# One decoder layer with two token mixers, on one core: C21's block product ahead of C12's, single-bank PSUM tiles, and the first MLP pair's operands made ahead

## The chip, the cores and the metric

The kernel runs on one core of a Trainium2 chip. The metric is the device time of one execution in microseconds (us). TensorE (PE) does the matmuls, VectorE (DVE) and ScalarE (ACT) the elementwise work, GpSimd (POOL) elementwise work on SBUF, and SyncE (SP) issues all the transfers of the parts treated here, in one queue and in order.

## The reference

One layer on x, 1024 positions by 1024 features, all in float32:

```python
h = rmsnorm(x, mix_norm)
q, k, v, su, sv, g_a, g_b = split(h @ w_in)
y_att = sliding_window_attention(q, k, v, q_norm, k_norm, sinks)
y_sgu = chunked_spatial_gating(su, sv, sgu_norm, w_s, b_s)
merged = sigmoid(g_a) * (y_att @ w_oa) + sigmoid(g_b) * (y_sgu @ w_ob)
x = x + merged @ w_out
z = rmsnorm(x, ffn_norm) @ w_up              # 1024 x 5632
zc = conv_b + three causal taps of z          # depthwise over positions
gate, val = split(zc)
x = x + (silu(gate) * val) @ w_down
```

## The kernel before

A float32 number is split into a high and a low part (h, l), so that one product of operands is three matmul passes: high by high, high by low, low by high. ACT makes the high part (`copy_hi`, L87), and DVE or POOL subtracts it from the value to get the low part (L984 and L1315 among others). The large products (the gates, `merged @ w_out`, the MLP's up and down projections) are moreover cut into 2x2 blocks, and are computed with seven products of blocks instead of eight, on sums of blocks: on the left A11, A12, A22 and the sums S1 to S4, on the right B11, B21, B22 and the sums T1 to T4.

TensorE's order is written out by hand; the other engines take their instructions in the order of the program. What a matmul waits for follows from its operands and its PSUM tile. PSUM has eight banks of 512 float32 columns. In the part that matters here four of them are two tiles of 128x1024 in the pool psA, and four are two such tiles in psC. `PS` hands out tiles from the rotating list `psum["P"]`, so that two tiles come from one pool and the next two from the other.

The stages, in order:

- **Gates.** `gate_pair(c, prev)` for c = 1 to 7 computes one block column of both gates in seven products (`Blocks.prod`, L1024, 12 matmuls each) and adds the partial sums with DVE. `gate_out` applies tanh and stores the result (`dth`); `last_sum` of the pair before and `scale` come first on DVE.
- **Sum units.** `sums_step` makes sums of weights that later stages read: a unit of kind "o" (four DVE adds of 128x256, of `wout`) or "u" (two of 128x512, of `wup`). A unit is a load into one of two buffers `ls`, the adds (L620), and a store of the result (L1089 or L1096). `UNITS` gives the order. The step also issues a later unit's load. These steps are called three times per gate pair and beside some of the branches.
- **Branches.** 16 jobs (`branch(n)`), each 24 matmuls (L91, L93) of an attention or gating output by a column block of `w_oa` or `w_ob` (`wj`), followed by a DVE product with the stored tanh (`th`, loaded by `th_load` two branches ahead).
- **Out stage.** 14 groups, two for each of the products M1 to M7 in `OUT`, each 24 matmuls (L1456) into four half tiles of `X` (psC) or `Yb` (psA). Behind a group, `main` adds, stores and splits: `half_add` (L1312) adds the residual block from `acs`, `end_c11`, `end_c22`, `end_c12` and `end_c21` finish one block of the new x each, and make the right operands of the MLP from it (`hi`, `lo`, `lo_gain`). `ahead` issues what later groups and the first MLP pair need.
- **MLP.** 22 pairs: pair n computes a gate and a value column of 128 with the seven products, then the convolution (L1525), tanh and product (L1548, L1549). `first_pair` is written out on its own, as it starts on operands that the out stage is just finishing; its products stood in the order A11B11, S1T1, S3T3, A12B21, S2T2, S4B22, A22T4. The second pair's product A11B11 and the sums of squares for the RMS norm (L1504) follow, then `fast_pair` for the rest.
- **Down projection.** `mms` (L1812), again seven products in groups, into four tiles `pd` (`X`, the pool psD, which takes the banks of psC) and four half tiles `pdy` (`Yb`, psA).

Of the kernel before, what the change touches and what calls it, by code (L numbers as in the profile page):

```python
# [41 lines left out]
def body(ctx, tc, nc, a):  # L42
# [103 lines left out]
    psA = ctx.enter_context(tc.tile_pool(name="psA", bufs=2, space=bass.MemoryType.PSUM, reuse_waits="tile"))  # L146
# [977 lines left out]
    def gate_pair(c, prev):  # L1124
# [16 lines left out]
        sums_step()  # L1141
# [15 lines left out]
        sums_step()  # L1157
# [15 lines left out]
        if c > 1:  # L1173
            sums_step()
# [43 lines left out]
    def branch(n):  # L1218
        br, c = B_ORDER[n]

        def main(w):
# [16 lines left out]
            if n % 2 == 0 or n in (5, 9):  # L1238
                sums_step()
# [3 lines left out]
    def m_split(n, ks, src):  # L1243
        if n not in rt:
            rt[n] = (U if n in ("B21", "B22") else Y)("r" + n, R, [128, 2, 4, 512])
        copy_hi(rt[n][:, 0, ks, :], src)
        nc.vector.tensor_tensor(rt[n][:, 1, ks, :], src, rt[n][:, 0, ks, :].bitcast(F), op=ALU.subtract)
# [21 lines left out]
    for n in range(16):  # L1269
# [4 lines left out]
    OUT = (("M1", "B11", 0), ("M2", "B21", 1), ("M6", "T2", 0), ("M7", "T3", 2), ("M5", "T1", 3), ("M3", "B22", 1),  # L1274
           ("M4", "T4", 3))
# [5 lines left out]
    def open_out():  # L1281
# [8 lines left out]
        pools["ng2"] = fp.tile([128, 8], F, name="ng2")  # L1290
        nc.vector.tensor_scalar(pools["ng2"], g2, -1.0, None, op0=ALU.mult)
# [47 lines left out]
    def copies():  # L1339
        for d in range(4):  # L1340
            nc.scalar.copy(Yb[d], X[d])

    def end_c11():
        t = acs["C11"]
        for d in range(4):
            half_add(Yb[d], Yb[d], t[:, d, :])
            nc.scalar.copy(t[:, d, :], Yb[d])
            x2_store("C11", d)
            hi("B11", d, Yb[d], gain(d))
            if d:  # L1350
                lo_gain("B11", d - 1, Yb[d - 1], gain(d - 1))
        lo_gain("B11", 3, Yb[3], gain(3))
# [4 lines left out]
    def end_c22():  # L1357
        t = acs["C22"]
        sqt = Y("sqt", F, [128, 2, 4, 512])[:, 0]
        sq2 = pools["sq2"][:, H]  # L1360
        for d in range(4):
# [3 lines left out]
            nc.scalar.activation(sqt[:, d, :] if d else sq2, t[:, d, :], AF.Square)  # L1365
            if d:
                nc.gpsimd.tensor_tensor(sq2, sq2, sqt[:, d, :], op=ALU.add)
        for d in range(4):
            lo_gain("B22", d, t[:, d, :], gain(4 + d))

# [5 lines left out]
    def end_c12():  # L1376
        t, h11, h22 = acs["C12"], acs["C11"], acs["C22"]
        tr = Y("traw", F, [128, 2, 4, 512])
        traw.append(tr)

        def late(d):
            lo("T1", d, X[d])
            nc.vector.tensor_tensor(tr[:, 1, d, :], h22[:, d, :], X[d], op=ALU.subtract)  # L1383
# [603 lines left out]
```

## Time and profile before

| | |
|---|---|
| median of 3 runs | 1236.7 us (1235.47 to 1239.26) |
| profiled execution | 1236.46 us, span 1234.8 us |
| granted TensorE clock, mean | 0.987 |
| busy: PE, DVE, ACT, POOL | 96%, 75%, 46%, 48% of the span |
| stages | gate pairs 246.6 to 394.7, branches to 487.6, out stage to 572.3, first pair to 612.2, down projection from 1019.1 |

Times in the trace are counted from the start of the span. An engine's row has its start, its duration, the line of the code, the operation with output and inputs, the tile shapes and the number of instructions merged into the row; in brackets stands the idle time before it, and what ended that.

### The profile page before, as it was taken

How to read it: one execution, taken by the hardware profiler on the slowest of the kernel's cores; microseconds unless marked ns; L12 is line 12 of the kernel's file. 1: busy time of each engine (PE TensorE's matmuls, PEld its weight loads, DVE VectorE, ACT ScalarE, POOL GpSimd, SP SyncE). 2: the span in 40 equal slices, each digit the busy share in tenths (PEclk: the TensorE clock that was granted, in tenths of full speed). 3: DMA queues.
4: the chain of work that ended last, by engine and by line, in shares of the span. 5: the costliest groups of instructions: out<-in, count | busy, mean ns of one | idle time of the engine just before them, and what ended most of it. 6: DMA issues, size and time to landing. Idle time of an engine off the chain costs nothing.

```text
span 1234.8 us, 16059 instructions
## 1 busy us (share of the span) xinstructions
PE 1180.9 (96%) x5842; PEld 995.3 (81%) x5842; DVE 932.0 (75%) x1094; ACT 568.0 (46%) x882; POOL 592.9 (48%) x375
## 2 busy tenths in 40 slices
PE   8999999999997899987699999999999999999998
PEld 8999889888876788775578888888888888788887
DVE  8789966688757677596478887788878888875674
ACT  8565558643334212555444544444444435434332
POOL 2467674587585223366457566575665642000000
PEclk9999999999998999999899999999999999999999
DMA  7010152267866998561223342342332447985372
GB/s 278 19 53 18 53 181 76 87 218 265 303 216 234 339 321 302 187 209 64 70 84 127 108 141 96 109 144 102 130 110 96 145 162 244 384 274 188 122 234 79
DMA packets 92767, 202.82 MB, mean 164 GB/s; under 512 B 9744, under 2 KB 18192, under 8 KB 92688
## 3 DMA queue, kind: packets, MB, share of 16 engines
q1 hardware_dynamic: 92688, 201.80, 47.5%
q8 instruction: 46, 0.75, 0.2%
q14 instruction: 33, 0.27, 0.1%
HBM read 146.97 MB, written 54.79 MB: 163 GB/s over the span
## 4 chain that ended last, share of the span: by engine, by line
PE 48%; DVE 2%; ACT 1%; issue 1%; ACTq 0%; DVEq 0%
PE pz L1024 31%; PE pd L1812 9%; PE pdy L1812 7%; DVE sq L1337 0%; DVE res L1832 0%; DVE tg L1525 0%; DVE pz L1040 0%; ACT tv L1520 0%; DVE tt L620 0%; PE pz L138 0%; ACT px L1336 0%; PE pz L1504 0%; DVE tv L1525 0%; DVE pz L1548 0%; DVE tv L1549 0%
## 5 line engine op out<-in xcount | busy, mean ns | idle before, releaser
L1024 PE MATMUL pz<-T,qh 128*128 128x512 f32 x472 | 147.1, 393 | 5.7 <-DVE traw L1383 2.8
L984 POOL TENSOR_TENSOR pl<-lp,ph 128x1024 fp32r<-128x1024 f32 x30 | 73.8, 2459 | 81.5 <-ACT ph L87 81.5
L1024 PE MATMUL pz<-B,ph 128*128 128x512 f32 x352 | 109.6, 392 | 2.3 <-DVE traw L1383 1.5
L1024 PEld LDWEIGHTS pz<-T,qh 128*128 128x128 f32 x472 | 88.9, 189 | 26.0 <-ACT AX L87 3.2
L1024 PE MATMUL pz<-T,ql 128*128 128x512 f32 x236 | 92.3, 391 | 0.0
L1024 PE MATMUL pz<-T,s3h 128*128 128x512 f32 x232 | 72.6, 395 | 12.7 <-ACT tmp L1598 12.7
L1024 PEld LDWEIGHTS pz<-B,ph 128*128 128x128 f32 x352 | 65.1, 188 | 18.4 <-ACT x L1656 3.5
L984 POOL TENSOR_TENSOR ql<-lq,qh 128x1024 fp32r<-128x1024 f32 x30 | 77.7, 2590 | 3.9 <-ACT qh L87 3.9
L1040 DVE TENSOR_TENSOR pz<-pz,rstd_b 128x1024 f32<-128x1024 f32 x60 | 73.9, 1232 | 7.4 <-ACT rstd_b L141 5.4
L620 DVE TENSOR_TENSOR ls<-ls 128x512 f32<-128x512 f32 (+1 forms) x60 | 58.5, 975 | 25.5 <-DMA ls<-wup 16.0
L984 POOL TENSOR_TENSOR s3l<-s,s3h 128x512 fp32r<-128x512 f32 x29 | 38.3, 1320 | 68.1 <-ACT s3h L87 68.1
L1024 PE MATMUL pz<-B,pl 128*128 128x512 f32 x176 | 68.6, 390 | 0.0
L1812 PE MATMUL pd<-bl,ah 128*128 128x512 f32 x176 | 68.5, 389 | 0.0
L1812 PE MATMUL pd<-bh,ah 128*128 128x512 f32 x176 | 68.5, 389 | 0.0
L1812 PE MATMUL pd<-bh,al 128*128 128x512 f32 x176 | 68.5, 389 | 0.0
L1024 PE MATMUL pz<-T,AX 128*128 128x512 f32 x264 | 63.4, 389 | 0.0
L1024 PE MATMUL pz<-B,AX 128*128 128x512 f32 x264 | 63.4, 389 | 0.0
L1024 PEld LDWEIGHTS pz<-T,s3h 128*128 128x128 f32 x232 | 44.2, 191 | 22.3 <-ACT tmp L1598 13.1
L1024 PEld LDWEIGHTS pz<-B,AX 128*128 128x128 f32 x264 | 49.6, 188 | 10.3
L1024 PEld LDWEIGHTS pz<-T,AX 128*128 128x128 f32 x264 | 49.5, 188 | 10.3
L1525 DVE SCALAR_TENSOR_TENSOR tv<-pz,cp,tv 128x1023 f32<-128x1023 f32 (+1 forms) x44 | 56.2, 1278 | 0.8
L1525 DVE SCALAR_TENSOR_TENSOR tg<-pz,cp,tg 128x1023 f32<-128x1023 f32 (+1 forms) x44 | 56.2, 1278 | 0.8
(361 smaller groups left out, 3559.9 us busy)
## 6 DMA issues: line engine op xcount, KB each, us to landing
lp<-wup SPq DMA_DIRECT2D x22, 512.0 KB, 3.6
ra<-wdown SPq DMA_DIRECT2D x44, 256.0 KB, 4.9
b<-T SPq DMA_DIRECT2D x44, 256.0 KB, 4.0
ls<-wup SPq DMA_DIRECT2D x18, 512.0 KB, 6.2
sum<-ls SPq DMA_DIRECT2D x18, 512.0 KB, 6.3
B<-tv SPq DMA_DIRECT2D x33, 256.0 KB, 2.3
T<-tt SPq DMA_DIRECT2D x33, 256.0 KB, 2.0
b<-B SPq DMA_DIRECT2D x33, 256.0 KB, 3.3
```

The costliest lines, as they stand in the source:

```text
L620: eng.tensor_tensor(out, x, y, op=op)
L984: nc.gpsimd.tensor_tensor(l, r, h.bitcast(F), op=ALU.subtract)
L1024: nc.tensor.matmul(o, p[:, k, :], y[:, q, k, :], start=not more and k == 0 and j == 0, stop=k == 3 and j == 2, skip_group_check=True)
L1040: nc.vector.tensor_tensor(z, z, rstd_b, op=ALU.mult)
L1525: nc.vector.scalar_tensor_tensor(t[:, j:], p[:, 0:1024 - j], cw[:, ci, 2 - j:3 - j], t[:, j:], op0=ALU.mult, op1=ALU.add)
L1812: nc.tensor.matmul(o[d], p[:, k - k0, m], q[:, k - k0, :], start=new and k == 0 and j == 0, stop=k == HK - 1 and j == 2, skip_group_check= ...
```

## The change

- `UNITS` is in another order: the "o" units come earlier (two in each of the gate pairs 2 to 4). `gate_pair(7)` makes no unit, and the branches make one each except n = 7 and n = 15.
- In the out stage M4 (C21's last product) comes ahead of M3 (C12's last). `X` and `Yb` are eight tiles of one bank in new pools "x" and "y" (in place of psC and psA). M2 starts its banks afresh; C11's first part is added to the residual from X (`add_x`) instead of being copied to Yb. The right operands are prepared four groups ahead instead of two. Two right operands change place between the pools Y and U.
- What T1 and T3 of the MLP need of C11, C12's residual and C22 is put together in `w_c12` at groups 10 and 11; after M3 one DVE operation finishes each piece of T1 and T3 from X. POOL adds T2 from T3; `t2_split` and `t4_split` are run inside the first pair. The loads of the first pair's weights are issued at groups 8 and 9, their splits at 10 to 12.
- `first_pair` has the order A11B11, A12B21, S1T1, S3T3, S2T2, S4B22, A22T4. It opens new pools psA2 and psC2, takes its own two tiles from psA2, and the rotation list starts with psC2. `mlp` takes `pdy` from psA2.

In the changed code most lines stand 1 to 29 numbers further on: L1024 becomes L1025, L1456 L1485, L1548 L1577, L1812 L1839.

```diff
-    psA = ctx.enter_context(tc.tile_pool(name="psA", bufs=2, space=bass.MemoryType.PSUM, reuse_waits="tile"))
+    psum["A"] = tc.tile_pool(name="psA", bufs=2, space=bass.MemoryType.PSUM, reuse_waits="tile")
+    psA = psum["A"].__enter__()
...
     UNITS = [("o", 0), ("o", 1)]
-    for c in range(6):
-        UNITS += [("u", 2 * c), ("o", c + 2), ("u", 2 * c + 1)]
-    UNITS += [("u", i) for i in range(12, NPAIR)]
+    for c in range(3):
+        UNITS += [("o", 2 * c + 2), ("u", c), ("o", 2 * c + 3)]
+    UNITS += [("u", i) for i in range(3, NPAIR)]
...
         gate_out(("b", c - 1), prev.zg)
-        sums_step()
+        if nx:
+            sums_step()
         q.prod(q.v0, "S3", "T3")
...
             nx.sums_r()
-        sums_step()
+            sums_step()
         q.prod(q.v0, "A22", "T4", more=True)
...
         gate_out(("a", c), q.zv)
-        if c > 1:
+        if 1 < c < 6:
             sums_step()
         q.prod(q.g1, "S4", "B22", more=True)
...
-            if n % 2 == 0 or n in (5, 9):
+            if n % 8 != 7:
                 sums_step()
...
-            rt[n] = (U if n in ("B21", "B22") else Y)("r" + n, R, [128, 2, 4, 512])
+            rt[n] = (U if n in ("B21", "T4") else Y)("r" + n, R, [128, 2, 4, 512])
...
-    OUT = (("M1", "B11", 0), ("M2", "B21", 1), ("M6", "T2", 0), ("M7", "T3", 2), ("M5", "T1", 3), ("M3", "B22", 1),
-           ("M4", "T4", 3))
+    OUT = (("M1", "B11", 0), ("M2", "B21", 1), ("M6", "T2", 0), ("M7", "T3", 2), ("M5", "T1", 3), ("M4", "T4", 3),
+           ("M3", "B22", 1))
...
-        for o, pool in ((X, psum["Cp"]), (Yb, psA)):
-            for _ in range(2):
-                p = pool.tile([128, 1024], F, tag="P", name=nm("px"))
-                o.extend([p[:, L], p[:, H]])
+        psum["C"].__exit__(None, None, None)
+        psum["A"].__exit__(None, None, None)
+        for o, n in ((Yb, "y"), (X, "x")):
+            psum[n] = tc.tile_pool(name="ps" + n, bufs=1, space=bass.MemoryType.PSUM, reuse_waits="tile")
+            pool = psum[n].__enter__()
+            o.extend(pool.tile([128, 512], F, tag=f"{n}{i}", name=f"px{n}{i}") for i in range(4))
...
-    def copies():
+    def add_x(n, o):
         for d in range(4):
-            nc.scalar.copy(Yb[d], X[d])
+            half_add(acs[n][:, d, :], o[d], acs[n][:, d, :])
...
+    def sq_c22():
+        sq2 = pools["sq2"][:, H]
+        for d in range(1, 4):
+            nc.gpsimd.tensor_tensor(sq2, sq2, traw[0][:, 1, d, :], op=ALU.add)
...
+    def w_c12(part):
+        t, tr = acs["C12"], traw[0]
+        for d in range(4):
+            if part == 0:
+                nc.vector.scalar_tensor_tensor(tr[:, 0, d, :], t[:, d, :], gain(d), acs["C11"][:, d, :],
+                                               op0=ALU.mult, op1=ALU.subtract)
+            else:
+                nc.scalar.activation(tr[:, 1, d, :], t[:, d, :], AF.Copy, scale=pools["ng"][:, d:d + 1])
+                nc.vector.scalar_tensor_tensor(tr[:, 1, d, :], acs["C22"][:, d, :], gain(4 + d), tr[:, 1, d, :],
+                                               op0=ALU.mult, op1=ALU.add)
+
+    def end_c21():
+        t = acs["C21"]
+        for d in range(4):
+            half_add(t[:, d, :], Yb[d], t[:, d, :])
+            x2_store("C21", d)
+            hi("B21", d, t[:, d, :], gain(4 + d))
+        for d in range(4):
+            lo_gain("B21", d, t[:, d, :], gain(4 + d))
+
     def end_c12():
-        t, h11, h22 = acs["C12"], acs["C11"], acs["C22"]
-        tr = Y("traw", F, [128, 2, 4, 512])
-        traw.append(tr)
-
-        def late(d):
-            lo("T1", d, X[d])
-            nc.vector.tensor_tensor(tr[:, 1, d, :], h22[:, d, :], X[d], op=ALU.subtract)
-            hi("T3", d, tr[:, 0, d, :])
-
+        tr = traw[0]
+
+        def t1(d):
+            nc.vector.scalar_tensor_tensor(tr[:, 0, d, :], X[d], pools["hg"][:, d:d + 1], tr[:, 0, d, :],
+                                           op0=ALU.mult, op1=ALU.add)
+            hi("T1", d, tr[:, 0, d, :])
+
+        def t3(d):
+            nc.vector.scalar_tensor_tensor(tr[:, 1, d, :], X[d], pools["nhg"][:, d:d + 1], tr[:, 1, d, :],
+                                           op0=ALU.mult, op1=ALU.add)
+            hi("T3", d, tr[:, 1, d, :])
+            lo("T3", d, tr[:, 1, d, :], nc.gpsimd)
+
+        def l1(d):
+            lo("T1", d, tr[:, 0, d, :])
+
+        def t2(d):
+            nc.gpsimd.tensor_tensor(tr[:, 0, d, :], tr[:, 1, d, :], acs["C11"][:, d, :], op=ALU.add)
+
+        t1(0)
+        t3(0)
+        for d in range(1, 4):
+            t1(d)
+            l1(d - 1)
+            t3(d)
+            t2(d - 1)
+        l1(3)
+        t2(3)
         for d in range(4):
-            half_add(X[d], X[d], t[:, d, :])
-            nc.scalar.copy(t[:, d, :], X[d])
+            half_add(acs["C12"][:, d, :], X[d], acs["C12"][:, d, :])
             x2_store("C12", d)
-            nc.vector.scalar_tensor_tensor(tr[:, 0, d, :], X[d], pools["ng2"][:, d:d + 1], h22[:, d, :],
-                                           op0=ALU.mult, op1=ALU.add)
-            nc.vector.scalar_tensor_tensor(X[d], X[d], gain(d), h11[:, d, :], op0=ALU.mult, op1=ALU.subtract)
-            hi("T1", d, X[d])
+
+    def t2_split():
+        for d in range(4):
+            hi("T2", d, traw[0][:, 0, d, :])
+            lo("T2", d, traw[0][:, 0, d, :], nc.gpsimd)
+
+    def t4_split():
+        tr, t = traw[0], acs["C21"]
+        for d in range(5):
+            if d < 4:
+                nc.vector.scalar_tensor_tensor(tr[:, 0, d, :], t[:, d, :], gain(4 + d), tr[:, 0, d, :],
+                                               op0=ALU.mult, op1=ALU.subtract)
+                hi("T4", d, tr[:, 0, d, :])
             if d:
-                late(d - 1)
-        late(3)
-
-    def end_c21():
-        t, tr = acs["C21"], traw[0]
-
-        def late(d):
-            lo_gain("B21", d, Yb[d], gain(4 + d))
-            nc.vector.scalar_tensor_tensor(Yb[d], Yb[d], gain(4 + d), tr[:, 1, d, :], op0=ALU.mult, op1=ALU.subtract)
-            hi("T4", d, Yb[d])
-
-        for d in range(4):
-            half_add(Yb[d], Yb[d], t[:, d, :])
-            nc.scalar.copy(t[:, d, :], Yb[d])
-            x2_store("C21", d)
-            hi("B21", d, Yb[d], gain(4 + d))
-            if d:
-                late(d - 1)
-            if d > 1:
-                lo("T4", d - 2, Yb[d - 2])
-        late(3)
-        lo("T4", 2, Yb[2])
-        lo("T4", 3, Yb[3])
-        for d in range(4):
-            hi("T2", d, tr[:, 1, d, :])
-            lo("T2", d, tr[:, 1, d, :], nc.gpsimd)
+                lo("T4", d - 1, tr[:, 0, d - 1, :])
...
-                                         start=s in ("M1", "M7") and kp == 0 and k == 0 and j == 0,
+                                         start=s in ("M1", "M2", "M7") and kp == 0 and k == 0 and j == 0,
                                          stop=kp == 1 and k == 1 and j == 2, skip_group_check=True)
             yield
             if g == 6:
                 scaled("C11", 0)
+            if g in (1, 5, 7):
+                add_x(*{1: ("C11", X), 5: ("C21", X), 7: ("C22", Yb)}[g])
             if g == 10:
-                scaled("C22", 4)
-            ends = {1: copies, 3: end_c11, 9: end_c22, 11: end_c12, 13: end_c21}
+                w_c12(0)
+            ends = {3: end_c11, 9: end_c22, 11: end_c21, 13: end_c12}
             if g in ends:
                 ends[g]()
-            if g in (5, 7):
-                c, b = (("C21", X), ("C22", Yb))[g == 7]
-                for d in range(4):
-                    half_add(acs[c][:, d, :], b[d], acs[c][:, d, :])
-            if g == 12:
-                for d in range(4):
-                    lo("T3", d, traw[0][:, 0, d, :], nc.gpsimd)
 
         def ahead():
             w = lefts[0]
-            if g + 2 < 14:
-                m_prep(g + 2)
+            if g + 4 < 14:
+                m_prep(g + 4)
             for i in (2, 3) if g == 0 else (g + 3,):
                 if i < 14:
                     job_split(16 + i)
...
                     job_load(16 + i)
             if g in (2, 4, 6):
                 ac_load({2: "C21", 4: "C22", 6: "C12"}[g])
+            if g == 8:
+                w.load_p()
+                w.load_s3()
+            if g == 9:
+                w.load_q()
             if g == 10:
-                first_left()
+                w.split_p()
+                sq_c22()
             if g == 11:
-                w.split_p()
                 w.split_s3()
                 w.split_q()
+                w_c12(1)
             if g == 12:
                 w.sums_r()
-            if g == 13:
                 w.split_r(0)
...
     def first_pair():
         w, nx = lefts[0], lefts[1]
-        zv, zg = (psum["Cp"].tile([128, 1024], F, tag="P", name=nm("pz")) for _ in range(2))
-        psum["P"][:] = [psA, psA, psum["Cp"], psum["Cp"]]
+        for n in "xy":
+            psum[n].__exit__(None, None, None)
+        psA = psum["Ap"] = ctx.enter_context(tc.tile_pool(name="psA2", bufs=2, space=bass.MemoryType.PSUM,
+                                                          reuse_waits="tile"))
+        psum["C"] = tc.tile_pool(name="psC2", bufs=2, space=bass.MemoryType.PSUM, reuse_waits="tile")
+        psC = psum["C"].__enter__()
+        zv, zg = (psA.tile([128, 1024], F, tag="P", name=nm("pz")) for _ in range(2))
+        psum["P"][:] = [psC, psC, psA, psA]
         q = Pair(0, w.w, (zg, zv))
-        tmp = pools["fp"].tile([128, 4, 512], F, tag="ac", name="tmp", bufs=4)
-        x1, x7, u2, u5 = (tmp[:, i, :] for i in range(4))
-        q.u2 = u2
+        x1, x7, q.u2, u5 = (acs["C22"][:, i, :] for i in range(4))
         q.prod(q.v1, "A11", "B11")
         nc.scalar.copy(x1, q.v1)
         nx.load_p()
-        q.prod(q.g1, "S1", "T1")
-        nc.scalar.copy(u5, q.g1)
+        q.prod(q.g0, "A12", "B21")
         nx.load_q()
         nx.load_s3()
+        t2_split()
+        q.prod(q.g1, "S1", "T1")
+        t4_split()
+        nc.scalar.copy(u5, q.g1)
+        nc.vector.tensor_tensor(q.g0, x1, q.g0, op=ALU.add)
         q.prod(q.v0, "S3", "T3")
-        nc.vector.tensor_tensor(x7, u5, q.v0, op=ALU.add)
-        q.prod(q.g0, "A12", "B21")
-        nc.vector.tensor_tensor(q.g0, x1, q.g0, op=ALU.add)
         nx.split_p()
         nx.split_s3()
-        for d in range(4):
-            sq_add("C12", d, Yb[d])
         q.prod(q.v1, "S2", "T2", more=True)
-        nc.scalar.copy(u2, q.v1)
+        nc.vector.tensor_tensor(x7, u5, q.v0, op=ALU.add)
+        nc.scalar.copy(q.u2, q.v1)
         nc.vector.tensor_tensor(q.v1, x7, q.v1, op=ALU.add)
         for d in range(4):
-            sq_add("C21", d, Yb[d])
+            sq_add("C21", d, acs["C21"][:, d, :])
         q.prod(q.g1, "S4", "B22", more=True)
+        for d in range(4):
+            sq_add("C12", d, acs["C12"][:, d, :])
         nx.sums_r()
         nx.split_q()
         lefts[2].load_p()
         q.prod(q.v0, "A22", "T4", more=True)
-        nc.vector.tensor_tensor(q.v0, u2, q.v0, op=ALU.add)
+        nc.vector.tensor_tensor(q.v0, q.u2, q.v0, op=ALU.add)
         pools["ft_cm"] = tc.tile_pool(name="ft", bufs=1, reuse_waits="tile")
         q2 = Pair(1, nx.w)
...
             for _ in range(2):
-                p = psA.tile([128, 1024], F, tag="P", name=nm("pdy"))
+                p = psum["Ap"].tile([128, 1024], F, tag="P", name=nm("pdy"))
```

More of the change, by code (lines that the diff above doesn't have):

```diff
@@ L1289, in open_out @@
         pools["sq2"] = fp.tile([128, 1024], F, name="sq2")
-        pools["ng2"] = fp.tile([128, 8], F, name="ng2")
-        nc.vector.tensor_scalar(pools["ng2"], g2, -1.0, None, op0=ALU.mult)
+        for n, f in (("ng", -1.0), ("hg", 0.5), ("nhg", -0.5)):
+            pools[n] = fp.tile([128, 4], F, name=n)
+            nc.vector.tensor_scalar(pools[n], g2[:, 0:4], f, None, op0=ALU.mult)
         dr = pools["dr"]
@@ L1345, in end_c11 @@
         for d in range(4):
-            half_add(Yb[d], Yb[d], t[:, d, :])
-            nc.scalar.copy(t[:, d, :], Yb[d])
+            half_add(t[:, d, :], Yb[d], t[:, d, :])
             x2_store("C11", d)
-            hi("B11", d, Yb[d], gain(d))
-            if d:
-                lo_gain("B11", d - 1, Yb[d - 1], gain(d - 1))
-        lo_gain("B11", 3, Yb[3], gain(3))
+            hi("B11", d, t[:, d, :], gain(d))
+        for d in range(4):
+            lo_gain("B11", d, t[:, d, :], gain(d))
         nc.scalar.activation(pools["sq2"][:, L], t[:, 0, :], AF.Square)
@@ L1358, in end_c22 @@
         t = acs["C22"]
-        sqt = Y("sqt", F, [128, 2, 4, 512])[:, 0]
+        tr = Y("traw", F, [128, 2, 4, 512])
+        traw.append(tr)
         sq2 = pools["sq2"][:, H]
```

15 lines of the change are left out of this document (3 added, 12 removed).

## The prediction

> **What bounds the kernel now.** I read the page's head first, then a table of stretches, then TensorE's waits, then the timelines of the engines at each wait.
>
> ```profile
> span 1234.8 us, 16059 instructions
> ...
> PE 1180.9 (96%) x5842; PEld 995.3 (81%) x5842; DVE 932.0 (75%) x1094; ACT 568.0 (46%) x882; POOL 592.9 (48%) x375
> ```
>
> TensorE (PE) is busy for 1180.9 of 1234.8 us, so only what it waits for, and what runs slowly behind a wait, can be won or lost, as the change removes no product. The stretches are the last gate pairs, the 16 branches, the out stage (the seven products M1 to M7), and the first MLP pair with the first product of the second; after the span and PE's busy time come the other engines', then the granted clock and the DMA share.
>
> ```profile
> 342.60:394.74 52.14, 42.11 (x170) 33.35 (x168) 34.00 (x31) 20.35 (x25) 34.67 (x19) 0.93 0.73 248
> 394.74:487.58 92.84, 89.22 (x386) 73.06 (x384) 66.73 (x69) 16.53 (x25) 26.68 (x17) 0.98 0.86 303
> 487.58:572.33 84.75, 77.17 (x337) 62.67 (x336) 63.28 (x60) 48.78 (x67) 50.83 (x23) 1.00 0.52 174
> 572.33:614.88 42.55, 25.65 (x97) 19.98 (x97) 23.11 (x35) 20.74 (x35) 18.40 (x13) 0.80 0.21 74
> ```
>
> TensorE's waits between 240 and 630 us name what ended each (total, times, longest):
>
> ```profile
> PE pz L1024 <- ACT tmp L1598: 12.7, 1, 12.7
> PE pz L1024 <- ACT x L1136: 4.8, 1, 4.8
> PE pz L1024 <- DVE x L1154: 4.5, 1, 4.5
> PE pz L1024 <- DVE traw L1383: 4.4, 2, 2.8
> PE px L1456 <- DVE ac L1312: 3.4, 1, 3.4
> PE po L91 <- ACT wjh L87: 3.0, 1, 3.0
> PE px L1456 <- ACT px L1341: 2.2, 1, 2.2
> PE pz L1024 <- DVE pz L1614: 1.4, 1, 1.4
> ...
> PE po L93 <- POOL wjl L108: 0.6, 1, 0.6
> ...
> PE px L1456 <- DVE rT L1247: 0.4, 1, 0.4
> ```
>
> All the edits aim at waits in this list. The units of the sum come from TensorE's timeline (start, duration, instruction, and in brackets the idle time before it):
>
> ```profile
> 390.46 4.43 PE L1024 MATMUL pz<-x,gax 128*128 128x512 f32 x12 [4.46 <-DVE x L1154]
> ...
> 500.83 11.17 PE L1456 MATMUL px<-rB,we 128*128 128x512 f32 x48 [2.21 <-ACT px L1341]
> ...
> 568.81 1.97 PE L1456 MATMUL px<-rT,wl 128*128 128x512 f32 x8
> ...
> 602.30 2.88 PE L1024 MATMUL pz<-T,AX 128*128 128x512 f32 x12
> 605.02 2.88 PE L1024 MATMUL pz<-B,AX 128*128 128x512 f32 x12
> ...
> 614.88 1.84 PE L1504 MATMUL pz<-ones,sq 128*128 128x2 f32 x16
> ```
>
> A product of 12 matmuls takes 605.02 - 602.30 = 2.72 us in a row; behind the 4.46 us wait the same dozen lasts 4.43 instead of 2.88, a slow start of 1.55 us. A branch has 24 matmuls: 5.44 us.
>
> **Part 1, the sum units moved (gate stage and branches).** Each unit of sums_step is a load, adds on VectorE (DVE) and a store; an "o" unit has four adds of 256 columns, a "u" unit two of 512. The change makes more "o" units at the gate pairs c = 2 to 4, none in pair 7, and runs 14 units beside the branches instead of 10.
>
> ```profile
> 362.30 5.56 DVE L620 TENSOR_TENSOR ls<-ls 128x256 f32<-128x256 f32 x4 [4.43 <-DMA ls<-wout]
> ...
> 381.69 1.42 DVE L620 TENSOR_TENSOR ls<-ls 128x512 f32<-128x512 f32 x2 [6.64 <-DMA ls<-wup]
> ...
> 432.09 1.41 DVE L620 TENSOR_TENSOR ls<-ls 128x512 f32<-128x512 f32 x2
> ...
> 444.43 2.39 DVE L620 TENSOR_TENSOR ls<-ls 128x512 f32<-128x512 f32 x2 [1.73 <-DMA ls<-wup]
> ```
>
> The "o" unit at 362.30 stands ahead of the DVE work that TensorE's 4.8 us wait ends on; a "u" unit of 1.41 us takes its place, still behind its load: I take 1.3 us off this wait. The unit at 381.69, which had waited 6.64 us for its load, stands ahead of the add that ends the 4.46 us wait; pair 7 now has none, so this wait and the slow start behind it go: 6.0 us. The SP queue (which issues all transfers) shows the third place:
>
> ```profile
> SPq L1096 <- DVE ls L620: 8.4, 1, 8.4
> ```
>
> The store of pair 7's "o" unit waited 8.4 us for DVE, and the branch weights queued behind it came late: waits of 3.0 and 0.6 us. Without it the branch stage is its matmuls alone, 16 x 5.44 = 87.0 instead of 92.84: 5.8 us. Together 1.3 + 6.0 + 5.8 = 13.1 us.
>
> Two costs stand against it. Each of three gate pairs swaps a "u" for an "o", up to 5.56 - 1.41 = 4.1 us more of DVE time, 12.5 in all, ahead of the pair's own adds; most of it lies under TensorE's 19 us per pair, and I take 2.5 us (0 to 6). Next, the two buffers of the units form a ring: a unit's load waits until the store of the unit before last has landed, and on SP the th and weight loads queue behind that wait. The landing times in the branch stage:
>
> ```profile
> L1070 SPq DMA_DIRECT2D ls<-wup x10: 423/430/1139, 405.8 to 473.6; - x10
> ...
> DMA to landing us min/median/max: 4.0/5.8/7.1
> ```
>
> ```profile
> L1089 SPq DMA_DIRECT2D sum<-ls x10: 326/327/425, 406.7 to 478.1; - x10
> ...
> DMA to landing us min/median/max: 3.8/5.3/6.4
> ```
>
> Two units take a store, a load and 1.41 us of adds, by the medians (5.3 + 5.8 + 1.4) / 2 = 6.25 us a unit; the two units between 432.09 and 444.43 took 6.17 each. 14 units at 6.2 need 86.8 us, beside 87.0 of matmuls: just enough, but with 4 more units of 1.31 MB on the 28.1 MB that 303 GB/s over 92.84 us make, transfers land later. At 6.43 us a unit the stage is 3 us too long, which I take (0 to 8). Part 1: 13.1 - 2.5 - 3 = 7.6 us gained (0 to 13).
>
> **Part 2, the out stage.** M2 now starts fresh banks, so the copies of C11's tiles (ACT px L1341) go, and with them 2.2 us; operands prepared four groups ahead remove the 0.4 us behind rT. C21's product goes ahead of C12's: M4 follows M5 in banks that need no earlier add, while M3, which needs C22's half-adds gone from its banks, comes 11 us later, an out step being the 48 matmuls of the row at 500.83, so the 3.4 us (DVE ac L1312) go. With one bank to a tile, a matmul waits only for its own tile's reader. 6.0 us gained (4 to 6). The cover for the added adds is DVE's 84.75 - 63.28 = 21 us of free time in the stage.
>
> **Part 3, the first MLP pair.** In before the last matmul of M3 and M4 ends at 568.81 + 1.97 = 570.78, and the second pair's column sums (L1504) start at 614.88: 44.1 us for eight products, 21.8 us of matmuls. The 12.7 us wait is GpSimd (POOL) splitting T3 behind ACT work of the C21 block. The new order gives A11B11, A12B21, S1T1 and S3T3 back to back, 11 us in which T1 and T3, one add each away, are finished. Then T2 decides, all whose steps queue on POOL:
>
> ```profile
> 578.55 2.37 POOL L984 TENSOR_TENSOR AX<-lr,AX 128x1024 fp32r<-128x1024 f32 x1
> 593.30 4.97 POOL L1315 TENSOR_TENSOR T<-traw,T 128x512 fp32r<-128x512 f32 x4 [12.37 <-ACT T L87]
> ```
>
> ```profile
> 577.93 0.69 DVE L1312 SCALAR_TENSOR_TENSOR px<-px,ac 128x512 f32<-128x512 f32 x1
> ```
>
> From the end of M3: one split of AX (0.5 to 2.9), then twelve operations (four splits of T3, four sums t2, four splits of T2) at 1.24 by the row, 1.3 with issue: 2.9 + 15.6 = 18.5. S2T2 ends at 19.2. S4B22 writes beside an add that DVE makes behind T4's last step, which waits for that T2 split, as it overwrites it: 18.5 + about four operations of 0.69 = 21.2. S4B22 slow 4.4, to 25.6; A22T4 2.7, to 28.3; the next pair's first product, to 31.0. Gain 44.1 - 31.0 = 13.1 us (10 to 16). The rows show slow starts behind waits of 2.8 us and more; the clock column has 0.80 here. The Trainium skill ("TensorE: Matmul & The Clock Gate", Part 1) has the clock halved only after an idle window of about 3.4 us; by that S4B22 behind 2 us would not be slow, and the sum 1.55 us better.
>
> **Part 4, not in the change's words: the banks' parity.** The first pair now takes its two tiles from the pool psA2, and the rotation goes on with psC2; before it began in psC and went on with psA. Pairs alternate, so the last of 22 sat in psA, and now sits in psC2. The down projection's first product takes four banks from whichever pool psC leaves (psD). Before, these were the pair's before last, long free; now its first matmul waits until DVE's L1548 has read the last pair.
>
> ```profile
> 1019.14 0.39 PE L1812 MATMUL pd<-bh,ah 128*128 128x512 f32 x1
> ```
>
> ```profile
> 1033.95 1.23 DVE L1548 SCALAR_TENSOR_TENSOR pz<-pz,tg 128x1024 f32<-128x1024 f32 x1
> 1035.22 1.23 DVE L1549 TENSOR_TENSOR tv<-pz,tv 128x1024 f32<-128x1024 f32 x1
> ```
>
> ```profile
> PE pdy L1812 <- ACT pdy L1839: 1.7, 1, 1.7
> ```
>
> TensorE reaches the down projection at 1019.14 with no wait; L1548 ends at 1035.18. New wait 16.0 us, slow start 1.55, less the 1.7 us that it waits today in front of the second product (pdy), which is then covered: 15.9 us lost (14.5 to 18).
>
> **Sum.** 7.6 + 6.0 + 13.1 - 15.9 = 10.8 us faster. The profiled execution took 1236.46 us (span 1234.8), the median of the three is 1236.7: the two are one. 1236.46 - 10.8 = 1225.7 us.
>
> **Rivals.**
> (a) The ring is the bound. If load and store land at the slow end of their rows (7.1 + 6.4 + 1.4 = 14.9 for two), a unit takes 7.5 us, 14 of them 105, and the branches are 18 us late instead of 3: 1240.7 us, slower. It decides from 7.2 us a unit, where the whole gain is gone (14 x 7.2 = 100.8, 13.8 us late). For it: a DMA share of 0.86 with four units fewer. Against: PE never waited in the branches after 410, and two units in a row took 6.17 each.
> (b) POOL's chain is stretched by DVE's adds. This row has POOL's operation at a median of 1.74 us beside the pairs, against 1.24 above:
>
> ```profile
> L620 POOL TENSOR_TENSOR lr<-lq,lp x21: 1284/1737/1750, 607.1 to 995.7; 128x512 f32<-128x512 f32 x21
> ```
>
> Twelve operations x 0.44 put everything behind T2 5.3 us later: 1231.0 us. Against: the four at 593.30 took 1.24 although DVE had work near. The Trainium skill ("GPSIMD Engine Reference", Specifications) says that POOL's memory interface is shared with DVE and suffers from DVE instructions with two such inputs, which the T1 and T4 splits are; the 1.74 agrees with it, the 1.24 not.
> (c) The bank wait of part 4 does not come, the tiles being read earlier or the pools laid out otherwise: then 15.9 us more are won, 1209.8 us. For it only that the diff's words do not speak of it.
>
> **Chances.** Forecast 0.62, (a) 0.13, (b) 0.15, (c) 0.10. A measurement of this kernel tells about 0.3%, 3.7 us, from no change. Forecast and (b) lie mostly under 1233.0, and (c) does: faster 0.77. (a) straddles 1240.4: slower 0.11 with the worst ends of the forecast. Within: 0.12. The range 1210 to 1240 takes in (b), half of (c) and half of (a), and the bounds of part 1, the widest.
>
> **What would show it.** Right: no wait on px L1485 over 1 us; no "ACT tmp" wait; one wait of some 16 us at the first pd matmul (L1839), ended by DVE pz L1577, the longest of the kernel; M1 starting near 480 instead of 487.58; column sums 31 us behind the last out matmul; sum units 6 to 6.5 us apart. Wrong: units 7 us apart with PE waiting on wjh or th (a); POOL's T operations at 1.7 us (b); no wait in front of pd (c).

## The result

The changed kernel takes 1246.3 us (median of 4 runs, 1245.98 to 1247.95) against 1236.1 us of the kernel before (4 runs, 1234.99 to 1239.26): ratio 1.0081, 95% interval 1.006 to 1.0102. It is slower by 0.8% where the forecast was faster by 0.9%, and lies outside the forecast's range. The head of the profile of one execution (1247.95 us, the longest of the four):

```profile
span 1246.2 us, 16043 instructions
...
PE 1188.0 (95%) x5842; PEld 996.1 (80%) x5842; DVE 942.7 (76%) x1104; ACT 560.0 (45%) x866; POOL 597.8 (48%) x379
```

The same moments in both traces (timelines of TensorE, us from the start) show where each gain came and went. T0 stands for the end of the last out matmul:

| moment | before | after | ahead of before |
|---|---|---|---|
| branches start | 394.7 | 387.3 | 7.4 |
| M1 starts | 487.6 | 481.0 | 6.6 |
| M2 starts | 500.8 | 500.1 | 0.7 |
| last out matmul ends (T0) | 570.8 | 566.3 | 4.4 |
| first column sums (T0 + 44.1, T0 + 43.1) | 614.9 | 609.4 | 5.5 |
| last pair ends | 1019.3 | 1015.4 | 3.9 |
| first down matmul | 1019.1 | 1031.2 | -12.1 |
| end of the span | 1234.8 | 1246.2 | -11.4 |

TensorE's waits of the changed kernel, between 240 and 640 us and then from 990 us on:

```profile
PE pz L1025 <- DVE T L1320: 4.6, 4, 2.0
PE pz L1025 <- DVE pz L1632: 3.7, 1, 3.7
PE pxx L1485 <- POOL wol L1469: 3.4, 2, 1.7
PE pz L1025 <- ACT x L1137: 2.5, 1, 2.5
PE pz L1025 <- POOL T L1320: 2.5, 4, 0.8
...
PE po L91 <- ACT wjh L87: 2.1, 2, 1.1
```

```profile
PE pd L1839 <- DVE pz L1577: 15.9, 1, 15.9
```

The longest waits that the change aimed at are gone (tmp 12.7, ac 3.4 in the out stage, x L1154 4.5; the one on wjh is still there, with 2.1 us), and no new one but the last is long. But the first MLP pair is now slow in many small waits, and M1, which had none, waits for its weights. The stretches of branches, M1, the rest of the out stage (M2 to T0), and the first pair up to the column sums; then M2 to T0 in the kernel before:

```profile
387.31:481.03 93.72, 90.18 (x385) 72.67 (x383) 58.17 (x64) 15.09 (x23) 24.09 (x17) 0.98 0.87 294
481.03:500.13 19.10, 14.70 (x48) 10.96 (x49) 12.61 (x13) 4.87 (x6) 6.39 (x3) 0.82 0.81 280
500.13:566.34 66.21, 66.06 (x289) 53.63 (x287) 62.64 (x55) 35.69 (x47) 40.71 (x18) 1.00 0.56 186
566.34:609.40 43.06, 29.29 (x97) 20.36 (x98) 38.04 (x43) 21.86 (x35) 35.08 (x21) 0.88 0.27 92
```

```profile
500.83:570.78 69.95, 66.13 (x288) 53.82 (x288) 52.32 (x50) 41.80 (x58) 41.85 (x19) 1.00 0.46 157
```

M1 takes 19.1 us instead of 11 (clock 0.82). From M2 to T0 TensorE no longer waits (busy 66.1 of 66.2 us), and VectorE, with 10 us more work, is busy 62.6 of these 66.2 us, where before it was busy 52.3 of 70.0: it has hardly any slack left, and its queue runs late at the stage's end. The SP queue's waits (380 to 500 us) and VectorE's sum units in the branches show what held M1's weights, and the timeline of VectorE and GpSimd what holds the first pair. The first row is the change's, the second the kernel's before (390 to 490 us):

```profile
SPq L1070 <- DMA sum<-ls: 44.7, 12, 5.7
```

```profile
SPq L1069 <- DMA sum<-ls: 27.7, 9, 5.9
```

```profile
399.70 1.80 DVE L621 TENSOR_TENSOR ls<-ls 128x512 f32<-128x512 f32 x2
...
484.28 1.42 DVE L621 TENSOR_TENSOR ls<-ls 128x512 f32<-128x512 f32 x2 [7.12 <-DMA ls<-wup]
...
491.12 2.29 DVE L621 TENSOR_TENSOR ls<-ls 128x512 f32<-128x512 f32 x2 [1.63 <-DMA ls<-wup]
```

```profile
552.97 7.04 DVE L1387 SCALAR_TENSOR_TENSOR traw<-ac,cp,ac 128x512 f32<-128x512 f32 x4
559.93 1.78 DVE L1391 SCALAR_TENSOR_TENSOR traw<-ac,cp,traw 128x512 f32<-128x512 f32 x1
...
565.35 1.46 DVE L1391 SCALAR_TENSOR_TENSOR traw<-ac,cp,traw 128x512 f32<-128x512 f32 x1 [0.24 <-ACT traw L1390]
...
569.12 4.75 DVE L1323 SCALAR_TENSOR_TENSOR B<-ac,cp,B 128x512 fp32r<-128x512 f32 x4
573.79 0.74 DVE L1407 SCALAR_TENSOR_TENSOR traw<-pxx,hg,traw 128x512 f32<-128x512 f32 x1
```

```profile
588.02 5.88 POOL L1320 TENSOR_TENSOR T<-traw,T 128x512 fp32r<-128x512 f32 x4
```

From 399.70 to 491.12 stand 14 units, 13 intervals of 7.03 us on average. SP spent 44.7 us (27.7 before) waiting for unit stores to land, with the out weights queued behind. And at T0, 566.3, VectorE is only about to start C21's end; T1's first operation comes at 573.8, T0 + 7.5.

### The profile page after: what moved, and what is told of

Same layout as the page of the kernel before. It is cut to its first block, busy times and chain, and to the rows that moved or that the text cites. A ratio compares the mean times of both kernels' runs of the same rounds, so it can differ in the third digit from the quotient of the medians.

```text
span 1246.2 us, 16043 instructions
## 1 busy us (share of the span) xinstructions
PE 1188.0 (95%) x5842; PEld 996.1 (80%) x5842; DVE 942.7 (76%) x1104; ACT 560.0 (45%) x866; POOL 597.8 (48%) x379
## 4 chain that ended last, share of the span: by engine, by line
PE 56%; DVE 17%; DMA 8%; issue 6%; POOL 5%; ACT 3%; SPq 1%; ACTq 0%; POOLq 0%; DVEq 0%
PE pz L1025 33%; PE pd L1839 10%; PE pdy L1839 7%; DMA sum<-ls 3%; DMA ls<-wup 2%; DVE lsy L621 1%; DVE pz L1041 1%; DVE ls L621 1%; DMA wo<-so 1%; DVE xa L621 1%; DVE tv L1554 1%; DVE tg L1554 1%; DVE tt L621 1%; DVE sq L1342 1%; DVE ya L530 1%
## 5 line engine op out<-in xcount | busy, mean ns | idle before, releaser
L1025 PE MATMUL pz<-T,qh 128*128 128x512 f32 x472 | 147.5, 392 | 8.7 <-DVE T L1320 4.6
L1025 PEld LDWEIGHTS pz<-T,qh 128*128 128x128 f32 x472 | 88.4, 188 | 30.7 <-DVE T L1320 6.2
L1025 PE MATMUL pz<-B,ph 128*128 128x512 f32 x352 | 109.8, 393 | 3.1 <-DVE ac L1317 1.8
L1025 PE MATMUL pz<-T,ql 128*128 128x512 f32 x236 | 92.1, 390 | 0.0
L1839 PE MATMUL pd<-bh,ah 128*128 128x512 f32 x176 | 69.2, 393 | 15.9 <-DVE pz L1577 15.9
L621 DVE TENSOR_TENSOR ls<-ls 128x512 f32<-128x512 f32 (+1 forms) x58 | 51.8, 894 | 40.0 <-DMA ls<-wup 28.6
L1025 PEld LDWEIGHTS pz<-B,ph 128*128 128x128 f32 x352 | 65.1, 188 | 19.8 <-ACT x L1683 3.5
L1025 PE MATMUL pz<-T,s3h 128*128 128x512 f32 x232 | 72.6, 394 | 0.0
L985 POOL TENSOR_TENSOR s3l<-s,s3h 128x512 fp32r<-128x512 f32 x29 | 39.1, 1347 | 67.5 <-ACT s3h L87 67.5
L1025 PE MATMUL pz<-B,AX 128*128 128x512 f32 x264 | 66.0, 400 | 3.7 <-DVE pz L1632 3.7
L1839 PE MATMUL pd<-bh,al 128*128 128x512 f32 x176 | 69.0, 392 | 0.0
L1839 PE MATMUL pd<-bl,ah 128*128 128x512 f32 x176 | 68.9, 392 | 0.0
L1025 PE MATMUL pz<-B,pl 128*128 128x512 f32 x176 | 68.6, 390 | 0.0
L1025 PE MATMUL pz<-T,AX 128*128 128x512 f32 x264 | 64.6, 391 | 2.5 <-POOL T L1320 2.5
L1025 PEld LDWEIGHTS pz<-B,AX 128*128 128x128 f32 x264 | 51.1, 194 | 15.0 <-DVE pz L1632 4.2
L1025 PEld LDWEIGHTS pz<-T,AX 128*128 128x128 f32 x264 | 49.2, 188 | 14.2 <-POOL T L1320 4.2
L985 POOL TENSOR_TENSOR AX<-lr,AX 128x1024 fp32r<-128x1024 f32 x22 | 53.8, 2447 | 5.8 <-ACT AX L87 5.8
```

The lines of the kernel that those rows point to most:

```text
L621: eng.tensor_tensor(out, x, y, op=op)
L985: nc.gpsimd.tensor_tensor(l, r, h.bitcast(F), op=ALU.subtract)
L1025: nc.tensor.matmul(o, p[:, k, :], y[:, q, k, :], start=not more and k == 0 and j == 0, stop=k == 3 and j == 2, skip_group_check=True)
L1839: nc.tensor.matmul(o[d], p[:, k - k0, m], q[:, k - k0, :], start=new and k == 0 and j == 0, stop=k == HK - 1 and j == 2, skip_group_check= ...
```

## The experiments

**The banks' parity.** e1 lets X of the down projection take psA2's tiles, and Yb the banks of psC:

```diff
-            X.extend(ps.tile([128, 512], F, tag=f"pd{i}", name=f"pd{i}") for i in range(4))
+            Yb.extend(ps.tile([128, 512], F, tag=f"pd{i}", name=f"pdy{i}") for i in range(4))
             for _ in range(2):
-                p = psum["Ap"].tile([128, 1024], F, tag="P", name=nm("pdy"))
-                Yb.extend([p[:, L], p[:, H]])
+                p = psum["Ap"].tile([128, 1024], F, tag="P", name=nm("pd"))
+                X.extend([p[:, L], p[:, H]])
```

> The changed kernel with one edit: in the down projection X (pd) takes the two tiles of psA2 and Yb (pdy) the four banks of psC, so that the first product's banks are those of the pair before last. Theory (the parity of the banks costs a wait of its own): the 15.9 us wait at the first pd matmul goes, a wait of at most 2 us may stand in front of pdy: 1246.3 - 15.9 - 1.5 (slow start) + 1.7 = 1230.6 us, within 1.5. Rival (the last pair's DVE tail is needed at that point in any case): another wait of about 16 us takes its place, 1246 us.

Measured 1229.5 us (ratio to before 0.9938, 0.9912 to 0.9963): 16.7 us less than the change. The only wait left from 990 us on in e1:

```profile
PE pdy L1839 <- ACT pdy L1866: 0.4, 1, 0.4
```

So part 4 of the prediction is shown, in place and size; the rest of the change alone is faster than before. Up to the down projection e1 does what the change does, and yet its T0 is 564.5, 1.8 us earlier, and the stretch from T0 to the column sums 38.9 us against 43.1: by so much do single profiles of the same code differ there.

**The sum units.** e4 undoes their move (old order and places), in the changed kernel:

> The changed kernel with the order and the places of the sum units as before the change (units in pair 7, 10 in the branches). Theory (the moved units won 7.4 us in the gates and lost 6.7 us in the branches and 8.1 us in the first out product): branches start near 394.7, first out product near 487.6 with no wait on woh or wol, 11 us long: the last out matmul at 487.6 + 77.2 = 564.8 instead of 566.3, so 1244 to 1245 us, or less by up to 6 us if DVE's lateness at the out stage's start reached the first MLP pair. Rival (the late out weights come from the out stage's own preparation): the waits of the first out product stay, 1253 us.

Measured 1244.1 us (1.0057, 1.0034 to 1.0081), 2.2 us under the change; branches start at 394.1, M1 at 487.0, T0 at 563.3. The stretches of M1 and of the rest of the out stage in e4:

```profile
487.00:497.80 10.80, 10.80 (x49) 8.97 (x48) 9.84 (x10) 5.66 (x7) 7.61 (x3) 1.00 0.89 281
497.80:563.30 65.50, 65.50 (x290) 54.23 (x289) 61.92 (x56) 36.50 (x49) 40.70 (x17) 1.00 0.51 174
```

M1 has no wait, and M1 to T0 is 76.3 us against 83.2 before: here the out-stage edits bring 6.9 us, as part 2 had it. In the change's profile the moved units win 7.4 us up to the branches and are 3.0 us behind e4 at T0. That difference is not clear of the spread, nor are the 2.2 us of the medians, whose intervals overlap. M6, the product behind M2, starts at 511.5 in the change, at 506.3 to 510.7 in the four other runs with the same code up to there (e1, e3, e5, e9), and at 508.7 and 508.4 in the two with the old units (e4, e8). So the moved units win 7 us ahead of the branches, and by M6 nothing that is clear of this spread.

e2 adds a third buffer for the units, e6 (on e1) moreover issues their loads two ahead; the last line, at the end of the gates, is in e6 alone:

```diff
+        if n > 15 and n % 3 == 0:
+            return pools["l3"].tile([128, 1536], F, tag="l3", name=nm("ls"), bufs=1)
         return pools["ls"].tile([128, 1536], F, tag="ls", name=nm("ls"), bufs=2)
...
+        sums_load()
```

> The changed kernel with one edit: from the branches on the sum units have a third buffer, so that a unit's load waits for the store three units back. Theory (the ring of two sets the 7.0 us per unit, the SP queue stands behind it, and the out weights come late): units at 5.4 to 6 us, SP's wait on sums stores falls from 44.7 us to under 15, the branch stage 87 to 89 us instead of 93.7, the first out product 11 to 13 us instead of 19.1: 10 to 14 us faster, 1232 to 1236 us; if DVE's lateness at the end of the branches is also what delays the first MLP pair, up to 6 us more. Rival (the transfers' rate is the limit: 29.5 MB in the stage): the units stay near 7 us, 1244 to 1246 us.

> The kernel of e1 with three buffers for the sum units from the branches on, and each unit's load issued two units ahead instead of one (one more load at the end of the gates). Theory (a unit's load is issued only behind the store of the unit before, so that store and load stand one behind the other; e2's third buffer alone could not change that): units 5.4 to 5.8 us apart, hardly a DVE wait on ls, branches 87 to 88 us, the first out product 11 to 12 us long without waits on wol, the last out matmul near 552 to 555 us instead of 564.5: 1229.5 - 10 = 1218 to 1221 us. Rival (the transfers' rate is the limit): units still 6.4 us or more apart and out weights late, 1227 to 1230 us.

e2: 1242.7 us (1.0045, 1.0029 to 1.0061); e6: 1225.3 us (0.9909, 0.988 to 0.9939). Each wins some 4 us on its kernel in the median, with intervals that touch or overlap, and less than expected. In e2 the branches are 87.7 us, as their matmuls want, and M1 still 15.8 (475.6 to 491.4); in e6 they are 92.1 and 15.9, where 87 to 88 and 11 to 12 were expected. In e2 SP now waits for VectorE to finish the unit whose store is next (first row, e2), where in e6 it waits for stores again, and VectorE for th (rows two and three):

```profile
SPq L1092 <- DVE ls L621: 37.4, 12, 6.3
```

```profile
SPq L1072 <- DMA sum<-ls: 38.6, 11, 5.3
```

```profile
DVE m L1239 <- DMA th<-dth: 14.3, 4, 9.4
```

e10 and e13 have 12 and 13 units beside the branches (on e6): a third one in pair 6, and in e10 one in pair 7 (there `if nx:` in front of one `sums_step()` goes). The cut shows the step behind `gate_out(("a", c), ...)` and the branches' condition, which in e13 is `n not in (3, 7, 15)`. e14 (on e6) issues the units' transfers from ScalarE's queue (`nc.scalar.dma_start` for them).

```diff
-        if 1 < c < 6:
+        if 1 < c < 7:
...
-            if n % 8 != 7:
+            if n % 4 != 3:
```

> The kernel of e6 with 12 instead of 14 units beside the branches (a third one in pair 6, one in pair 7). Theory (the transfers' rate and the SP queue's order are at their limit with 14): out weights on time, the first out product 11 to 12 us instead of 15.3, hardly a wait on th; a wait of 0 to 3 us comes back in the last gate pair: 1220 to 1224 us. Rival (the late out weights have nothing to do with the count): 1225 to 1228 us.

> The kernel of e6 with 13 units beside the branches: pair 6 makes a third one, pair 7 none. Theory (the count beside the branches decides, and a unit in pair 7 brings back the wait at its last product: 5.2 us and a slow start in e10): branches start at 387 to 389 us, the out weights come nearly on time, the last out matmul at 554 to 557 us instead of 559 to 561: 1218 to 1221 us, faster than e10. Rival (whatever is won at the gates is given back, since the same transfers must be done by the out stage): the last out matmul at 559 to 561 us again, 1222 to 1225 us.

> The kernel of e6 with the loads and stores of the units beside the branches issued from ScalarE's queue instead of SP's. Theory (order: the th, wj and wo loads are late because they stand on SP behind a unit's load that waits for a store): the waits on th (14.3 us in total on VectorE in e6) and on wol (3.4 us) go, the last out matmul at 552 to 556 us instead of 560.6: 1219 us. Rival (rate: the transfers of 14 units and the branches' own fill the stage, whichever queue issues them): wol waits and th waits stay, or ScalarE's copies of wj come late instead, 1224 us or more.

e10: 1221.8 us (0.988, 0.9865 to 0.9895), the fastest kernel here; e13: 1224.5 (0.9902, 0.9882 to 0.9923), their intervals overlap. In e10 the branches and M1 are free of waits, but pair 7's one unit brings its wait back:

```profile
395.40:482.80 87.40, 87.40 (x385) 72.36 (x384) 58.73 (x64) 15.38 (x23) 24.19 (x17) 1.00 0.90 328
482.80:493.70 10.90, 10.90 (x49) 9.02 (x49) 9.90 (x11) 5.61 (x6) 7.61 (x3) 1.00 0.86 279
```

```profile
PE pz L1025 <- DVE x L1160: 5.2, 1, 5.2
```

T0 is 559.2 in e10, 557.2 in e13, 560.6 in e6, although their branches start at 395.4, 388.5 and 387.2: most of what is won ahead of the branches is given back by M1, the rival's reading. Yet e10 moves 328 GB/s in the branches against 294 in the change, so on average the change's stage was below a rate that the transfers reach here. That points to the order in the queue rather than to the amount, but does not show it. e14 was to separate the two and did not: 1240.8 us (1.0029, 1.0002 to 1.0055), branches of 113.6 us, since ScalarE now stands behind the units itself, and its copies of the branch weights with it (ScalarE's waits, 387 to 500 us):

```profile
ACT wjh L87 <- DVE ls L621: 32.9, 4, 11.7
```

Whether a queue that nothing else stands in would bring back what the branches and M1 lose stays open.

**The first MLP pair.** e3 leaves out `sq_c22` (GpSimd's sums of squares ahead of w_c12's second part), so the RMS norm of its MLP lacks most of C22's squares. e9 (on e1) keeps GpSimd quiet there.

> The changed kernel without the GpSimd sums of C22's squares at group 10 (sq_c22), so that the RMS norm of the MLP lacks three quarters of C22's squares. Theory (w_c12's second part waits behind them, as it overwrites the squares, and DVE's adds beside them are slow): T1's operands come 3 to 5 us earlier, and the stretch from the last out matmul to the column sums is 41 us instead of 45.3: 1242 to 1243 us. Rival (DVE's own queue of out-stage work sets T1, and GpSimd is beside the point): under 1 us.

> The kernel of e1 with GpSimd quiet at the end of the out stage: the first MLP pair's weights get a copy of themselves (ScalarE) as low part instead of GpSimd's difference, and C22's squares are left out of the RMS norm, so the numbers of the MLP change. Theory (VectorE's eight w_c12 operations, with two inputs from SBUF, take 1.46 to 1.76 us each only because GpSimd works beside them): they take about 0.75 us, T1's first operation starts 5 to 8 us earlier (at the last out matmul + 0 to 2 us instead of + 4 to 7), the column sums 33 to 35 us behind the last out matmul instead of 38.9: 1224 us. Rival (that is what such an operation costs): w_c12 stays at 1.5 to 1.8 us, the column sums at 37 us or more, 1228 to 1230 us.

e3: 1246.5 us (1.007, 1.0047 to 1.0092), no gain; w_c12's second four took 7.97 us even so. T0 to the column sums was 42.0 us. e9: 1227.6 us (0.9924, 0.99 to 0.9948), 2 us under e1, and their intervals overlap; 37.5 us from T0 to the column sums against 38.9 in e1. Its VectorE rows, with GpSimd idle from 555.4 to 562.2:

```profile
548.29 5.95 DVE L1392 SCALAR_TENSOR_TENSOR traw<-ac,cp,ac 128x512 f32<-128x512 f32 x4
554.54 3.39 DVE L1396 SCALAR_TENSOR_TENSOR traw<-ac,cp,traw 128x512 f32<-128x512 f32 x4 [0.30 <-ACT traw L1395]
...
565.03 0.74 DVE L1412 SCALAR_TENSOR_TENSOR traw<-pxx,hg,traw 128x512 f32<-128x512 f32 x1
```

The second four take 0.85 us each with GpSimd idle, where they took 1.46 to 1.78 beside it (the first four, beside GpSimd until 555.4, still 1.49). T1 starts at T0 + 2.2 (T0 is 562.8) instead of T0 + 4.0 in e1, 1.8 us earlier and not the 5 to 8 of the theory, and the column sums come 1.4 us earlier. From T1's first operation to the column sums it is 35.3 us here, 34.9 in e1, 35.5 in e4 and 35.6 in the change: the chain behind T1 is long by itself, and these runs differ in when T1 starts (T0 + 4.4 in e4, T0 + 7.5 in the change).

e5 (on e1), e11 (on e6) and, with e10's edits, e12 take T2 off GpSimd, and move some adds in VectorE's order:

```diff
-            nc.gpsimd.tensor_tensor(tr[:, 0, d, :], tr[:, 1, d, :], acs["C11"][:, d, :], op=ALU.add)
+            nc.vector.tensor_tensor(tr[:, 0, d, :], tr[:, 1, d, :], acs["C11"][:, d, :], op=ALU.add)
...
-            lo("T2", d, traw[0][:, 0, d, :], nc.gpsimd)
+            lo("T2", d, traw[0][:, 0, d, :])
```

> The kernel of e1 with the first MLP pair's T2 taken off GpSimd: the sums for T2 and its low parts on VectorE, the add of x1 to g0 ahead of T2's and T4's splits, C12's half-adds behind T4. Theory (the GpSimd queue of twelve operations after T1 and T3, and then the add queued behind T4, hold S2T2 and S4B22): S2T2 ends about 20 us behind the last out matmul instead of 24 to 27, the 3.7 us wait of S4B22 goes with its slow start, the column sums start 32 to 35 us behind the last out matmul instead of 39 to 43: 1229.5 - 6 = 1223 to 1224 us. Rival (VectorE is the bound there and gets eight more operations in front of T1 and T4): column sums still 39 us or more behind, 1229 to 1232 us.

> The kernel of e6 with T2 on VectorE as in e5, but the add of x1 to g0 behind T2's split, so that S1T1, which writes the same tile, does not wait for it (12.7 us in e5), and C12's half-adds behind the adds that A22T4 waits for. Theory (e5 showed only that wait): column sums 33 to 35 us behind the last out matmul instead of 39.2, 1225.3 - 5 = 1220 us. Rival (VectorE's queue is the bound whichever way its work is ordered): 38 us or more, 1225 us.

> The edits of e10 and e11 together. If both theories hold: 1216 to 1218 us; if neither, 1225 us or more.

e5: 1230.2 us (0.9951, 0.9929 to 0.9974), e11: 1228.8 (0.994, 0.9922 to 0.9958), e12: 1224.4 (0.9901, 0.9886 to 0.9916): no gain, and in the medians e11 and e12 lose some 3 us against e6 and e10, with intervals that overlap. e5 made S1T1 wait 12.7 us for an add to the other half of its own tile:

```profile
585.15 1.22 PE L1025 MATMUL pz<-T,qh 128*128 128x512 f32 x2 [12.71 <-DVE pz L1630]
```

e11 removed that, and T0 to the column sums stayed 39.1 us (39.2 in e6). With T2 on VectorE, VectorE is late instead of GpSimd: the rival fits. e7 is e5 with e6's edits, e8 is e5 with the old units:

> The edits of e5 and e6 together on the kernel of e1. If both theories hold, their gains add: about 1213 us. If VectorE's queue at the end of the out stage is one cause for both, less: 1217 us.

> The kernel of e5 with the sum units in the places and order they had before the change. If the moved units cost what e4 showed (2 us in the median), this is 2 us faster than e5, near 1221 us; if e4's difference came from elsewhere, the same as e5.

e7: 1229.4 us (0.9935, 0.9913 to 0.9957), e8: 1228.4 (0.9931, 0.991 to 0.9951). e7 missed both of its values: the gains do not add. e8 is 1.8 us under e5, with overlapping intervals, as e4 was 2.2 under the change: these runs do not settle a difference of 2 us.

## Why the prediction was wrong

Part 4 was right: 15.9 us forecast, a wait of 15.9 and 16.7 us back in e1. Part 2's mechanism was right: 6.0 forecast, 6.9 from M1 to T0 in e4. Two terms were mis-sized: part 1 with its 8.1 us in M1 came to -1.5 us instead of 7.6, part 3 to 1.0 instead of 13.1. These 9.1 and 12.1 us are nearly all of the 22.2 us between 10.8 us faster and the spans' 11.4 slower; of the small rest, 1.6 us between the column sums and the last pair's end stays unexplained. The change's figures are read from one profile; in e1, the same code up to the down projection, part 3 came to 5.2, still 8 us short.

Part 1 was forecast at 7.6 us. It held up to M1 (6.6; 7.4 at the gates, where 4.8 were forecast), but the step "at 6.43 us a unit the stage is 3 us too long" failed: units came 7.03 us apart, the branches were 93.7 us instead of 87.0, and M1, whose weights stand behind the units' loads on SP, lost another 8.1 (19.1 instead of 11): 14.8 us instead of 3. This was rival (a), at a pace just under the 7.2 us that the prediction called decisive; what the rival lacked was that the delay goes on into M1. The prediction had taken the pace of pairs of units in the old schedule. That SP could catch up between them there, and with only two of 16 branches without a unit no longer can, fits the waits for stores (27.7 us before, 44.7 now), but no run isolates it.

Part 3 was forecast at 13.1 us and brought 1.0 (T0 + 44.1 to T0 + 43.1). The step that failed is "then T2 decides, all whose steps queue on POOL", with the chain that was put at 31.0 us from T0. First, the chain was begun as if VectorE were free at T0, but T1 began at T0 + 7.5. The out stage's cover of "21 us of free time" on VectorE was gone: from M1 to T0 in e4 VectorE is busy 71.7 of 76.3 us (61.7 of 83.2 before), as the stage is shorter and has 10 us more VectorE work. Here the eight w_c12 operations took 13.2 us (7.04 + 1.78 + three of 1.46) and would take some 6.8, an estimate, at e9's 0.85 with GpSimd idle. Second, the chain behind T1 took 35.6 us, as in e1, e4 and e9, so that even with T1 at T0 the forecast was 4.6 us too short. T2's last split ended at T0 + 27.6 (forecast 18.5), S4B22 started at T0 + 32.1 (21.2) and took 5.5 us (4.4).

Rival (b) came in part. GpSimd's twelve operations, from 576.08 to 593.90, took 17.8 us instead of 15.6: four of them 1.66 to 1.73 each, which is (b)'s sign, four 1.26 to 1.29, the last four 1.47 (588.02). By the estimate above the larger cost was on the other engine: VectorE's w_c12 operations doubled. The Trainium skill's rule ("GPSIMD Engine Reference", Specifications) is borne out by this: w_c12 has two inputs from SBUF and slowed, while T1's first operation, with one input from PSUM, took 0.74 us. What the prediction held against (b), the 1.24 of the row at 593.30, does not count: VectorE was idle beside most of it, from 594.0 to 599.8.

```profile
599.83 0.69 DVE L1605 TENSOR_TENSOR tmp<-tmp,pz 128x512 f32<-128x512 f32 x1 [5.81 <-PE pz L1024]
```

That row was also misread: it holds T2's splits, as T3's had ended at 578.6. The 12.7 us wait of S3T3 ended with ScalarE's copy of x1 (L1598) out of the tile that S3T3 writes, queued behind ScalarE's work for C21. The new order removes it either way, so the forecast did not suffer by this.

The Trainium skill's other rule ("TensorE: Matmul & The Clock Gate", Part 1: half clock after about 3.4 us idle) was weighed on a wait that came out longer: S4B22 waited 3.75 us and was slow (5.49 us for 12 matmuls), as both the rule and the rows have it. Two other places do not fit it, nor the prediction's "waits of 2.8 us and more". In the change's M1, matmuls ran slow behind waits of 1.0 and 1.69 us (1.05 us for two, where 0.62 is usual); in the kernel before, 48 matmuls behind a wait of 3.42 us were not slow:

```profile
492.19 0.80 PE L1485 MATMUL pxx<-rB,wol 128*128 128x512 f32 x1 [1.69 <-POOL wol L1469]
492.78 1.05 PE L1485 MATMUL pxx<-rB,woh 128*128 128x512 f32 x2
```

```profile
548.76 11.15 PE L1456 MATMUL px<-rB,we 128*128 128x512 f32 x48 [3.42 <-DVE ac L1312]
```

So the length of the last wait alone does not decide it here, and in this kernel the measured rows go before the rule.

The chance of slower was put at 0.11, mostly from rival (a); the misses of parts 1 and 3 are of the same kind, a queue near its limit taken as free.

## What to carry to other kernels

When TensorE's stalls are taken out of a stage, recount the busy time of the engine that feeds it, with the work added, against the shorter stage: 52 us of VectorE in 70 left room, 63 in 66 did not, and what stands behind the stage starts from its queue. A transfer put into an in-order queue costs what stands behind it, two stages on if need be. And when tiles change pools, follow the rotation to the program's last user of each bank: here a swap of two pools cost 16 us at the one place where the next stage takes the banks.

## What the runs showed of the hardware

A VectorE operation (scalar_tensor_tensor) of 128x512 with two inputs from SBUF took 0.85 us with GpSimd idle (e9) and 1.46 to 1.78 beside GpSimd's two-input operations (the change), while the same kind of operation with one input from PSUM took 0.74 beside them. The change's own trace has both cases on one line, L1445: two operations of 1.72 us beside GpSimd's splits, which end at 593.9, and two of 0.74 behind them. In the branches, 328 GB/s were moved without a wait (e10), in a stage that at 294 GB/s had been late (the change).
